# Layer 0's network: key weights staged in sixteen half tiles over two buffers, in the third part and its down part

## The chip, the cores and the metric

The kernel runs on one core of a Trainium2 chip. Its time is device microseconds of one execution; a version is run several times and stands for the median. A core has five engines that run their own instruction streams in order and wait for each other by semaphores: PE (TensorE, matrix products), DVE (VectorE), ACT (ScalarE), POOL (GpSimd) and SP (SyncE). Data moves between memory (DRAM) and the on-chip memory (SBUF) by DMA transfers, which SP, ACT and POOL issue and 16 DMA engines carry out. Products are summed up in PSUM banks.

## The reference

A trunk of two layers over 512 tokens of 1024 features, all float32. Layer 0 is a Mamba-2 mixer and a convolutional feed-forward network (the "network" of the title); then come shared keys and values; layer 1 is differential attention and a second network. What matters here:

```python
def conv_ffn(x, ln_g, up_w, conv_w, conv_b, down_w):
    u = causal_dwconv(rms_norm(x, ln_g) @ up_w, conv_w, conv_b)
    gate, up = u[..., :FFN_DIM], u[..., FFN_DIM:]          # FFN_DIM = 2816
    return (jax.nn.silu(gate) * up) @ down_w

def shared_kv(x, kv_ln_g, kv_w, k_norm_g):
    kv = rms_norm(x, kv_ln_g) @ kv_w
    k = kv[..., :K_DIM].reshape(b, s, ATT_HEADS, 2, ATT_HEAD_DIM)
    v = kv[..., K_DIM:].reshape(b, s, ATT_HEADS, ATT_V_DIM)
    return rms_norm(k, k_norm_g), v

for layer in range(2):
    mix = mamba2_mixer(...) if layer == 0 else diff_attention(x, k_sh, v_sh, ...)
    x = x + mix
    x = x + conv_ffn(x, ...)
```

The gain kv_ln_g of the norm ahead of the keys can be multiplied into the rows of the key half of kv_w beforehand: row k of kv_w times kv_ln_g[k]. That is what is staged here.

## The kernel before

**Products.** A float32 product is made of three PE products of rounded pieces: high piece times high piece, high times low, low times high. For each piece of weights of 128x1024 that comes by DMA (wr_h for the up weights, L177; wr_s, wz, wx for the down weights, L1245 and L1267), ACT copies the high piece wh (L185, L1276) and DVE subtracts to get the low piece wl (L196, L1277). The buffers of wr, wh and wl are three each, so ACT can make the piece of chunk k only when PE has done chunk k - 3.

**Layer 0's network.** Its 22 blocks of 128 gate and 128 up features are worked in three parts, blocks 0 to 5, 6 to 13 and 14 to 21. A plain block is two steps (P), each one chunk of up weights (h_p_0, h_p_1) with 24 matmuls of 128x512; its results are tapped by the convolution (ACT L1066, DVE L1068), pass the Silu on ACT (L1478) and are multiplied on DVE (L1160). In the second part four blocks are worked as doubles, two blocks by seven products (the digits in the list of steps). When a part is done, its share of the down product is made while the next part is under way: the letter D, the *down part*.

```python
PARTS_D = (0, 6), (6, 14), (14, 22)
STEPS = "PPPPPPPPPPPP", "PPDPP51P26P734P51P26734", "PPDPPPPPPPPPPPPPP"
```

The down part of layer 0 (down_features) is seven products, "5126743", each for two halves c of the output, so 14 chunks s_6_0, s_6_1, ... of 24 or fewer matmuls of 128x256. After each product DVE adds the bank ps_s into xT (L1417). For some products the weights are a sum of two quarters of the weight matrix: POOL issues an accumulating DMA (plus, L1238) into the tile wx or wz that the high and low pieces have just been made of.

**Order.** PE's order is written by hand. The other engines' instructions are ordered by a scheduler, which can place an instruction far ahead of the spot where the code emits it, if what it reads is there. `tc.issue_after(x)` keeps what is emitted under it behind the instruction x. SP issues loads in its order, POOL the accumulating ones, ACT the stores of the staged tiles.

**Staging of the key weights.** Layer 1's key products read scaled key weights from a scratch tensor ks in DRAM. Layer 0 fills it: key_weights_in(n) loads two blocks of rows of half the columns of kv_w, 512 KB, into the tile stage (L1005, issued by SP); key_weights_out scales it in place, one ACT instruction per block of rows (L1011), and stores it to ks by a DMA that ACT issues (L1012). There are eight such tiles and one buffer, so each load waits for the store before it. stage() is called after each step of the second and third part, and every other call loads, every other one scales and stores. The scheduler has put all eight tiles earlier: from the end of the mixer's output projection to the middle of the network's first part, from 357 to 438 us of the span.

Of the kernel before, what the change touches and what calls it, by code (L numbers as in the profile page):

```python
# [9 lines left out]
F32 = mybir.dt.float32  # L10
# [8 lines left out]
P = 128  # L19
# [26 lines left out]
def trunk_kernel(ctx: ExitStack, tc, x, ssm_ln_g, ssm_in_w, ssm_conv_w, ssm_conv_b, ssm_dt_bias,  # L46
# [23 lines left out]
    def w_cols(w, k0, nk, c0, ncol):  # L70
        return w[k0 * P:(k0 + nk) * P, c0:c0 + ncol].rearrange("(k p) c -> p k c", p=P), nk, ncol
# [929 lines left out]
        return ks[k0 * P:(k0 + 2) * P, i * 512:(i + 1) * 512].rearrange("(k p) c -> p k c", p=P)  # L1001

    def key_weights_in(pl, n):
        v = pl.tile([P, 1024], F32, tag="stage", name="stage%d" % n, bufs=1).rearrange("p (k c) -> p k c", k=2)
        sync.dma_start(v, w_cols(kv_w, n // 2 * 2, 2, n % 2 * 512, 512)[0])  # L1005
        return n, v

    def key_weights_out(n, v):
        k0, i = n // 2 * 2, n % 2
        for k in range(2):  # L1010
            act.activation(v[:, k], v[:, k], AF.Copy, scale=c2[:, 32 + k0 + k:33 + k0 + k])  # L1011
        act.dma_start(key_weights(k0, i), v)  # L1012

    def bias_ranges(pl, behind):
        pl = pl.rearrange("p a t -> p (a t)")
# [16 lines left out]
    def ffn(l, norm, bp, gnext, nnext):  # L1032
        with (tc.tile_pool(name="ffn_h%d" % l, bufs=1) as hp, tc.tile_pool(name="ffn%d" % l, bufs=1) as fp,
# [129 lines left out]
            def double(p, sides):  # L1163

                uu, ug = [u_tile("u%d%d_%d" % (l, us[0], p)) for _ in range(2)][::1 - 2 * (us[0] % 2)]
                us[0] += 1
                banks = {}
                for m in "5126734":
                    wh, wl = chunk("U%d%s_%d" % (l, m, p))
                    opens = m in "512"  # L1170
                    kind = "y" if m in "53" else "z" if m == "2" else "x"
                    if opens:
                        if m == "1":
                            banks["x"] = [mm_bank("ps_U%s%d_%d_%d" % (m, l, p, b))[:, :256] for b in range(2)]
                        else:
                            t = aux_bank("ps_U%s%d_%d" % (m, l, p))
                            banks[kind] = [t[:, b * 256:(b + 1) * 256] for b in range(2)]
                            banks[kind + "t"] = t.rearrange("p (b t) -> p b t", b=2)
                    ps = banks[kind]
                    hs, ls = up_side(m)  # L1180
                    for b in range(2):
                        cols = slice(b * P, (b + 1) * P)
                        skip = not opens or (b > 0 and m != "1")
                        for k in range(4):
                            pe.matmul(ps[b], wh[:, k, cols], hs[:, k, :], start=not skip and k == 0, stop=False,
                                      skip_group_check=skip)
                            pe.matmul(ps[b], wh[:, k, cols], ls[:, k, :], start=False, stop=False,
                                      skip_group_check=skip)
                        for k in range(4):
                            pe.matmul(ps[b], wl[:, k, cols], hs[:, k, :], start=False, stop=k == 3,  # L1190
                                      skip_group_check=skip)
                        if m == "1":
                            act.activation(ug[:, b, :256], ps[b], AF.Copy)
                        elif m == "6":
                            act.activation(ug[:, b, 256:], ps[b], AF.Copy)
                        elif m == "7":
                            dve.tensor_tensor(out=uu[:, b, 256:], in0=uu[:, b, 256:], in1=ps[b], op=sub)
                        elif m == "4":
                            act.activation(uu[:, b, :256], ps[b], AF.Copy, scale=-1.0)
                    if m == "5":  # L1200
                        act.activation(uu[:, :, 256:], banks["yt"], AF.Copy, scale=-1.0)
                    elif m == "2":
                        dve.tensor_tensor(out=ug[:, :, :256], in0=banks["zt"], in1=ug[:, :, :256], op=ALU.add)
                    elif m == "3":
                        dve.tensor_tensor(out=ug[:, :, 256:], in0=banks["yt"], in1=ug[:, :, 256:], op=ALU.add)
                        ga = [taps(0, p + b, ug[:, b]) for b in range(2)]
                        for b in range(2):
                            act.activation(ga[b], ga[b], AF.Silu)
                    elif m == "4":
                        for b in range(2):  # L1210
                            gated(p + b, ga[b], taps(1, p + b, uu[:, b]), sides)
                    yield
# [193 lines left out]
            def down_features(p0, n, sides, last):  # L1406
# [18 lines left out]
                for m in SEVEN[0]:  # L1425
                    opens = m in "512"
                    for c in range(2):
                        wh, wl = chunk("s0%s_%d_%d" % (m, p0, c))
                        kind = "y" if m in "53" else "z" if m == "2" else "x"
                        if opens:  # L1430
                            banks[kind, c] = (mm_bank if m == "5" else aux_bank)("ps_s%s_%d_%d" % (m, p0, c))
                        v = halves(banks[kind, c])
                        for b in range(2):
                            for low in range(2):
                                for q in range(nq):
                                    h, w = (t[:, side[m], :] for t in sides[q][:2])
                                    cols = slice(b * P, (b + 1) * P)
                                    if low:
                                        pe.matmul(v[:, b], wl[:, q, cols], h, start=False, stop=q == nq - 1,  # L1439
                                                  skip_group_check=not opens or b > 0)  # L1440
                                        continue
                                    pe.matmul(v[:, b], wh[:, q, cols], h, start=opens and q + b == 0, stop=False,  # L1442
                                              skip_group_check=not opens or b > 0)
                                    pe.matmul(v[:, b], wh[:, q, cols], w, start=False, stop=False,  # L1444
                                              skip_group_check=not opens or b > 0)
                        if m == "5":
                            add(c, 1, 1, v, ALU.subtract)
                        elif m == "1":
                            add(c, 0, 0, v)
                        elif m == "2":  # L1450
                            add(c, 0, 0, v)
                            ended(c, 0, 0)
                        elif m == "6":
                            add(c, 0, 1, v)
                        elif m == "7":
                            add(c, 1, 1, v, ALU.subtract)
                            ended(c, 1, 1)
                        elif m == "4":
                            add(c, 1, 0, v, ALU.subtract)
                            ended(c, 1, 0)  # L1460
                        else:
                            add(c, 0, 1, v)
                            ended(c, 0, 1)

            down = down_tokens if nnext is None else down_features
            hooks = state["hooks"]
# [8 lines left out]

            def tapped(p, us):
                ga = taps(0, p, us[0])
                act.activation(ga, ga, AF.Silu)  # L1478
                return ga, taps(1, p, us[1])

            staged = {"n": 0, "at": 0, "v": None}

            def stage():

                staged["at"] += 1
                if staged["v"] and staged["at"] > 1:
                    key_weights_out(*staged["v"])
                    staged.update(v=None, at=0)
                elif not staged["v"] and staged["n"] < KB and staged["at"] > 1:
                    staged.update(v=key_weights_in(fp, staged["n"]), n=staged["n"] + 1, at=0)  # L1490

            def plain(p, sides):

# [7 lines left out]
                gated(p, ga, up, sides)  # L1501
                return ga

            sides = {}
            ps0, ps1 = [], []
            w0 = whole(0, ps0)
            next(w0)
# [49 lines left out]
            for i in range(1, len(parts)):  # L1557
# [23 lines left out]
                for kind, p, step in order:  # L1581
                    if kind == "D":
                        q0, m = parts[i - 1]
                        down(q0, m, [behind[q0 + 2 * j] for j in range(m // 2)], False)
                        gate(sides)
                        continue
                    if p not in gens:
# [2 lines left out]
                    if kind == "P" and step == 1:  # L1590
                        run(gens[p])
                        if p > p0:
                            gate(sides)
                    if not l:
                        stage()
            if staged["v"]:
                key_weights_out(*staged["v"])
            assert l or staged["n"] == KB
            p0, n = parts[-1]
            down(p0, n, [sides[p0 + 2 * j] for j in range(n // 2)], True)  # L1600

# [459 lines left out]
```

## Time and profile before

| | us |
|---|---|
| median of 3 runs | 1311.98 |
| lowest, highest run | 1311.8, 1312.6 |
| the profiled execution | 1313.06 |
| span of its instructions | 1311.4 |

The profile is of one execution. Its time is a little longer than the span from the first to the last instruction that the profile shows; the profiled execution is 1.08 us above the median, and its granted TensorE clock is 0.999 in the mean. Rows of the timeline have the start in us, the duration in us, the engine, the line and the operation, "out<-in", and in brackets the idle time before and what ended it. SPq, ACTq and POOLq rows are the issue of a DMA by that engine. A row of waits has the waiting engine and line, what it waited for, and us in total, times, longest. The chain of waits runs in order of time: start, duration, what. The table of windows has the stretch, its length, the busy time of each engine, the granted clock, the share of the 16 DMA engines and GB/s. A row of a DMA queue has packets, megabytes and its share of the DMA engines.

The staging in the timeline of ACT and SP (starts, us):

| | 1 | 2 | 3 | 4 | 5 | 6 | 7 | 8 |
|---|---|---|---|---|---|---|---|---|
| load issued by SP | 356.73 | 366.30 | 377.08 | 385.91 | 396.79 | 405.18 | 414.42 | 427.17 |
| store issued by ACT | 362.93 | 373.78 | 383.10 | 391.66 | 402.35 | 410.53 | 421.93 | 434.37 |

The down part inside the third part has its matmuls on PE from 574.0 to 614.2 us; before and after it stand the plain steps of the third part.

### The profile page before, as it was taken

To read this page: it belongs to the slowest core of one execution; us is meant where nothing else is said; L and a number is where in the kernel's file an instruction comes from. 1 tells how busy PE (TensorE), PEld (TensorE's weight loads), DVE (VectorE), ACT (ScalarE), POOL (GpSimd) and SP (SyncE) were. 2 spreads that over 40 slices of the span, in tenths; PEclk is the share of its full clock that TensorE was granted. 3 is DMA by queue.
4 is the path that set the end of the run, shared out by engine and by line. 5 is a ranking of instruction groups with operands and counts; after the bars stand their busy time and mean duration, and the time that the engine had idled before them with its cause. 6 is when DMAs were issued, how large, how long until landed. Compare 5 with 4: busy or idle time off the path is not lost.

```text
span 1311.4 us, 19077 instructions
## 1 busy us (share of the span) xinstructions
PE 1302.4 (99%) x7123; PEld 1110.4 (85%) x7123; DVE 1083.1 (83%) x1812; ACT 746.1 (57%) x1234; POOL 184.7 (14%) x212
## 2 busy tenths in 40 slices
PE   9999999999999999999999999999999999999998
PEld 8878888888888798999889888888888889988887
DVE  7989878889869886996778879798789977997776
ACT  6596554743367545653445667777656536643442
POOL 5230200300020411111002310000020030020001
PEclk9999999999999999999999999999999999999999
DMA  7553533532366696778337673222233586565325
GB/s 207 153 154 96 149 100 98 152 96 73 102 192 186 177 218 155 156 150 205 100 97 143 168 157 112 81 65 65 65 105 89 149 203 155 141 123 188 99 61 128
DMA packets 198589, 174.20 MB, mean 133 GB/s; under 512 B 7964, under 2 KB 172192, under 8 KB 198496
## 3 DMA queue, kind: packets, MB, share of 16 engines
q1 hardware_dynamic: 164336, 119.69, 30.7%
q0 software_dynamic: 30704, 47.99, 19.2%
q10 hardware_dynamic: 3456, 5.30, 1.2%
q8 instruction: 56, 0.92, 0.3%
q14 instruction: 37, 0.30, 0.1%
HBM read 166.51 MB, written 6.44 MB: 132 GB/s over the span
## 4 chain that ended last, share of the span: by engine, by line
PE 95%; DVE 3%; ACT 1%; DMA 0%; issue 0%; DVEq 0%; ACTq 0%
PE ps_in L246 5%; PE ps_in L248 5%; PE ps_in L247 5%; PE ps_g L248 5%; PE ps_g L246 4%; PE ps_g L247 4%; PE ps_u L246 4%; PE ps_u L247 4%; PE ps_u L248 4%; PE ps_s L1439 3%; PE ps_s L1444 3%; PE ps_s L1442 3%; PE ps_s L1338 3%; PE ps_s L1341 3%; PE ps_s L1343 3%; PE ps_o L247 2%
## 5 line engine op out<-in xcount | busy, mean ns | idle before, releaser
L246 PE MATMUL ps_in<-xgh,wh_in 128*128 128x512 f32 x304 | 122.9, 404 | 0.0
L196 DVE TENSOR_TENSOR wl_h<-wr_h,wh_h 128x1024 fp32r<-128x1024 f32 x72 | 88.3, 1231 | 41.1 <-ACT wh_h L185 38.3
L248 PE MATMUL ps_in<-xgh,wl_in 128*128 128x512 f32 x304 | 119.8, 394 | 0.0
L247 PE MATMUL ps_in<-xgl,wh_in 128*128 128x512 f32 x304 | 119.2, 392 | 0.0
L248 PE MATMUL ps_g<-xgh,wl_h 128*128 128x512 f32 x288 | 112.7, 391 | 2.8 <-DVE wl_h L196 2.8
L247 PE MATMUL ps_g<-xgl,wh_h 128*128 128x512 f32 x288 | 113.0, 392 | 0.2 <-DVE xgl L1084 0.2
L246 PE MATMUL ps_g<-xgh,wh_h 128*128 128x512 f32 x288 | 113.2, 393 | 0.0
L247 PE MATMUL ps_u<-xgl,wh_h 128*128 128x512 f32 x288 | 112.1, 389 | 0.0
L246 PE MATMUL ps_u<-xgh,wh_h 128*128 128x512 f32 x288 | 112.1, 389 | 0.0
L248 PE MATMUL ps_u<-xgh,wl_h 128*128 128x512 f32 x288 | 112.0, 389 | 0.0
L185 ACT ACTIVATE wh_h<-wr_h 128x1024 fp32r<-128x1024 f32 x72 | 76.2, 1058 | 60.0 <-PE ps_u L247 17.8
L1083 ACT ACTIVATE sh<-vg 128x512 fp32r<-128x512 f32 (+1 forms) x81 | 42.2, 530 | 60.3 <-DVE vg L1160 35.5
L1238 POOL DMA_DIRECT2D wz<-in_ffn_down_w_dram x28 | 33.8, 1265 | 285.6 <-DVE wl_s L1277 131.0
L248 PEld LDWEIGHTS ps_in<-xgh,wl_in 128*128 128x128 f32 x304 | 57.1, 188 | 12.2 <-issue 0.4
L246 PEld LDWEIGHTS ps_in<-xgh,wh_in 128*128 128x128 f32 x304 | 57.2, 188 | 11.7 <-issue 1.3
L248 PEld LDWEIGHTS ps_g<-xgh,wl_h 128*128 128x128 f32 x288 | 54.5, 189 | 14.6 <-DVE wl_h L196 3.2
L247 PEld LDWEIGHTS ps_in<-xgl,wh_in 128*128 128x128 f32 x304 | 57.2, 188 | 11.0 <-issue 0.5
L247 PEld LDWEIGHTS ps_g<-xgl,wh_h 128*128 128x128 f32 x288 | 54.5, 189 | 11.5 <-DVE xgl L1084 0.6
L185 ACT ACTIVATE wh_in<-wr_in 128x1024 fp32r<-128x1024 f32 x39 | 41.2, 1057 | 40.2 <-PE ps_in L247 30.1
L1444 PE MATMUL ps_s<-sl,wh_s 128*128 128x256 f32 x252 | 64.1, 283 | 0.0
L1442 PE MATMUL ps_s<-sh,wh_s 128*128 128x256 f32 x252 | 64.1, 283 | 0.0
L246 PEld LDWEIGHTS ps_g<-xgh,wh_h 128*128 128x128 f32 x288 | 54.4, 189 | 11.0
(518 smaller groups left out, 3809.9 us busy)
## 6 DMA issues: line engine op xcount, KB each, us to landing
wr_h<-in_ffn_up_w_dram SPq DMA_DIRECT2D x60, 512.0 KB, 4.3
wr_in<-in_ssm_in_w_dram SPq DMA_DIRECT2D x40, 512.0 KB, 3.9
wz<-in_ffn_down_w_dram POOLq DMA_DIRECT2D x21, 512.0 KB, 6.8
m<-cumd POOLq DMA_DIRECT2D x16, 512.0 KB, 4.9
wr_out<-in_ssm_out_w_dram SPq DMA_DIRECT2D x16, 512.0 KB, 3.5
wr_s<-in_ffn_down_w_dram SPq DMA_DIRECT2D x13, 512.0 KB, 4.2
wr_h<-in_ffn_up_w_dram SPq DMA_DIRECT2D x24, 256.0 KB, 3.5
wx<-in_ffn_down_w_dram POOLq DMA_DIRECT2D x12, 512.0 KB, 7.4
```

The source lines that it names most:

```text
L185: return act.activation(self.wh[:, :self.n], self.raw[:, :self.n], AF.Copy)
L196: return eng.tensor_tensor(out=self.wl[:, :self.n], in0=self.raw[:, :self.n], in1=self.wh[:, :self.n].bitcast(F32), op=ALU.subtract)
L246: pe.matmul(ps, wh, xh, start=start, stop=False)
L247: pe.matmul(ps, wh, xl, start=False, stop=False)
L248: return pe.matmul(ps, wl, xh, start=False, stop=stop).ins
L1083: act.activation(hi, v, AF.Copy)
L1338: pe.matmul(pss[b], h, ws[q][1][:, cols], start=False, stop=end and q == qs[-1], skip_group_check=more)
L1341: pe.matmul(pss[b], h, ws[q][0][:, cols], start=first and q == qs[0], stop=False, skip_group_check=more)
L1343: pe.matmul(pss[b], w, ws[q][0][:, cols], start=False, stop=False, skip_group_check=more)
L1439: pe.matmul(v[:, b], wl[:, q, cols], h, start=False, stop=q == nq - 1, skip_group_check=not opens or b > 0)
L1442: pe.matmul(v[:, b], wh[:, q, cols], h, start=opens and q + b == 0, stop=False, skip_group_check=not opens or b > 0)
L1444: pe.matmul(v[:, b], wh[:, q, cols], w, start=False, stop=False, skip_group_check=not opens or b > 0)
```

## The change

There are sixteen half tiles of one block of rows and 512 columns (256 KB), over two buffers, in the place of eight tiles over one; the on-chip memory is the same. stage() is called in the third part alone: after each of its sixteen plain steps, and, by the new list `meanwhile`, after each product of its down part. The n-th call scales and stores half tile n - 2 and loads half tile n into the same buffer; scaling and store stand behind state["act"], the last ACT instruction noted at certain places (a product's evacuation in a double, or a Silu). Bytes and scalings are the same; loads and stores are sixteen each instead of eight.

```diff
     def key_weights_in(pl, n):
-        v = pl.tile([P, 1024], F32, tag="stage", name="stage%d" % n, bufs=1).rearrange("p (k c) -> p k c", k=2)
-        sync.dma_start(v, w_cols(kv_w, n // 2 * 2, 2, n % 2 * 512, 512)[0])
+        v = pl.tile([P, 512], F32, tag="stage", name="stage%d" % n, bufs=2)
+        sync.dma_start(v, w_cols(kv_w, n // 2, 1, n % 2 * 512, 512)[0].rearrange("p k c -> p (k c)"))
         return n, v
 
     def key_weights_out(n, v):
-        k0, i = n // 2 * 2, n % 2
-        for k in range(2):
-            act.activation(v[:, k], v[:, k], AF.Copy, scale=c2[:, 32 + k0 + k:33 + k0 + k])
-        act.dma_start(key_weights(k0, i), v)
+        k, i = n // 2, n % 2
+        act.activation(v, v, AF.Copy, scale=c2[:, 32 + k:33 + k])
+        act.dma_start(key_weights(k // 2 * 2, i)[:, k % 2], v)
...
                         if m == "1":
-                            act.activation(ug[:, b, :256], ps[b], AF.Copy)
+                            state["act"] = act.activation(ug[:, b, :256], ps[b], AF.Copy).ins
...
+                    for step in meanwhile:
+                        step()
...
             def tapped(p, us):
                 ga = taps(0, p, us[0])
-                act.activation(ga, ga, AF.Silu)
+                state["act"] = act.activation(ga, ga, AF.Silu).ins
                 return ga, taps(1, p, us[1])
 
-            staged = {"n": 0, "at": 0, "v": None}
+            staged = []
+            count = [0]
 
             def stage():
 
-                staged["at"] += 1
-                if staged["v"] and staged["at"] > 1:
-                    key_weights_out(*staged["v"])
-                    staged.update(v=None, at=0)
-                elif not staged["v"] and staged["n"] < KB and staged["at"] > 1:
-                    staged.update(v=key_weights_in(fp, staged["n"]), n=staged["n"] + 1, at=0)
+                n = count[0]
+                count[0] += 1
+                if 2 <= n < 2 * KB + 2:
+                    with tc.issue_after(state["act"]):
+                        key_weights_out(*staged.pop(0))
+                if n < 2 * KB:
+                    staged.append(key_weights_in(fp, n))
...
                     if kind == "D":
                         q0, m = parts[i - 1]
+                        meanwhile[:] = [stage] if not l and i == len(parts) - 1 else []
                         down(q0, m, [behind[q0 + 2 * j] for j in range(m // 2)], False)
+                        meanwhile[:] = []
                         gate(sides)
...
-                    if not l:
+                    if not l and i == len(parts) - 1:
                         stage()
```

In the changed file the lines of the network stand one further up or down: the scaling is L1010, the store L1011, the pieces wh_s L1275, the taps L1065, the Silu L1479.

What the scheduler makes of it. ACT's order in the first part, around the Silu of block 3 (vg_3; the numbers at the end of a name only tell tiles apart), before:

```order
L185 ACTIVATE wh_h_5_1_4120<-wr_h_5_1_4118 128x1024
L1066 ACTIVATE vg_4_4150<-ps_g_4_4084,cf_90 128x512
L1011 ACTIVATE stage_6225<-stage_6225,c_89 128x512 x2
L1478 ACTIVATE vg_3_4034<-vg_3_4034 128x512
L1012 DMA ks<-stage_6225 128x2x512
L1083 ACTIVATE sh_3959<-vg_3_4034 128x512
```

and now:

```order
L185 ACTIVATE wh_h_5_1_4120<-wr_h_5_1_4118 128x1024
L1065 ACTIVATE vg_4_4150<-ps_g_4_4084,cf_90 128x512
L1479 ACTIVATE vg_3_4034<-vg_3_4034 128x512
L1082 ACTIVATE sh_3959<-vg_3_4034 128x512
L185 ACTIVATE wh_h_6_0_4173<-wr_h_6_0_4171 128x1024
```

The two scalings and the store are gone from between vg_4 and the Silu of vg_3, as are the other staging rows of this part.

ACT's order in the down part inside the third part, from chunk 3 (the second wh_s row with wz_0 or wz_1 is chunk 9 or 8), before:

```order
L1276 ACTIVATE wh_s_6_1_5568<-wz_0_3669 128x1024
L1276 ACTIVATE wh_s_6_0_5601<-wr_s_6_0_5599 128x1024
L1276 ACTIVATE wh_s_6_1_5633<-wr_s_6_1_5631 128x1024
L1276 ACTIVATE wh_s_6_0_5663<-wx_1_3672 128x1024
L1276 ACTIVATE wh_s_6_1_5694<-wx_0_3671 128x1024
```

and now, from the same chunk to chunk 6:

```order
L1275 ACTIVATE wh_s_6_1_5542<-wz_0_3669 128x1024
L1010 ACTIVATE stage_5469<-stage_5469,c_89 128x512
L1010 ACTIVATE stage_5509<-stage_5509,c_89 128x512
L1011 DMA ks<-stage_5469 128x512
L1275 ACTIVATE wh_s_6_0_5579<-wr_s_6_0_5577 128x1024
L1011 DMA ks<-stage_5509 128x512
L1275 ACTIVATE wh_s_6_1_5611<-wr_s_6_1_5609 128x1024
L1010 ACTIVATE stage_5575<-stage_5575,c_89 128x512
L1011 DMA ks<-stage_5575 128x512
L1275 ACTIVATE wh_s_6_0_5645<-wx_1_3672 128x1024
```

Two scalings now stand ahead of chunk 4, and from chunk 6 to chunk 11 one scaling with its store ahead of each piece; the other eight scalings come in the plain steps of blocks 16 to 21.

SP's order over the same stretch, now (before, the same rows stood there without those of stage):

```order
L1266 DMA wr_s_6_0_5773<-in_ffn_down_w_dram 128x4x256
L1005 DMA stage_5575<-in_kv_w_dram 128x512
L1266 DMA wr_s_6_1_5806<-in_ffn_down_w_dram 128x4x256
L1005 DMA stage_5643<-in_kv_w_dram 128x512
L177 DMA wr_h_15_0_5907<-in_ffn_up_w_dram 128x8x128
L1005 DMA stage_5709<-in_kv_w_dram 128x512
L1005 DMA stage_5771<-in_kv_w_dram 128x512
L1005 DMA stage_5839<-in_kv_w_dram 128x512
L1244 DMA wz_1_3670<-in_ffn_down_w_dram 128x4x256
L1005 DMA stage_5905<-in_kv_w_dram 128x512
L1244 DMA wz_0_3669<-in_ffn_down_w_dram 128x4x256
L1005 DMA stage_5971<-in_kv_w_dram 128x512
```

Each of these loads of stage waits for the store of the half tile two before it, and the loads behind it wait with it. The first two loads of stage stand where the first one stood before, ahead of the first part. PE's and POOL's orders are unchanged.

More of the change, by code (lines that the diff above doesn't have):

```diff
@@ L1192, in double @@
                         if m == "1":
-                            act.activation(ug[:, b, :256], ps[b], AF.Copy)
+                            state["act"] = act.activation(ug[:, b, :256], ps[b], AF.Copy).ins
                         elif m == "6":
-                            act.activation(ug[:, b, 256:], ps[b], AF.Copy)
+                            state["act"] = act.activation(ug[:, b, 256:], ps[b], AF.Copy).ins
                         elif m == "7":
@@ L1502, in gate @@
                 return ga
-            sides = {}
+            sides, meanwhile = {}, []
             ps0, ps1 = [], []
@@ L1593, in ffn @@
                             gate(sides)
-                    if not l:
+                    if not l and i == len(parts) - 1:
                         stage()
-            if staged["v"]:
-                key_weights_out(*staged["v"])
-            assert l or staged["n"] == KB
+            assert l or (count[0] >= 2 * KB + 2 and not staged)
             p0, n = parts[-1]
```

## The prediction

> **What bounds the kernel now.** I read the page first: the span, the busy times, the shares of the chain that ended last.
>
> ```profile
> span 1311.4 us, 19077 instructions
> PE 1302.4 (99%) x7123; PEld 1110.4 (85%) x7123; DVE 1083.1 (83%) x1812; ACT 746.1 (57%) x1234; POOL 184.7 (14%) x212
> PE 95%; DVE 3%; ACT 1%; DMA 0%; issue 0%; DVEq 0%; ACTq 0%
> ```
>
> PE is busy 99% of the span and carries 95% of the chain. The diff gives PE the same instructions in the same order, so the time can move in two ways only: a wait of PE goes, or one comes. The view of PE's waits shows those it has, and the same view of everybody's waits from 340 to 440 us shows one that belongs to the staging:
>
> ```profile
> PE ps_g L248 <- DVE wl_h L196: 2.8, 1, 2.8
> ...
> ACT stage L1011 <- DMA stage<-in_kv_w_dram: 8.9, 3, 3.5
> ```
>
> PE's 2.8 us is the largest it has. The chain from 395 to 445 us says where it comes from:
>
> ```profile
> 427.17 5.47 DMA stage<-in_kv_w_dram
> 433.00 1.34 ACT stage L1011 x2
> 434.34 0.53 ACT vg L1478
> 435.50 1.23 DVE wl_h L196
> 436.78 0.50 PE ps_g L248
> ```
>
> The load of the last staged tile lands late, ACT has its two scalings ahead of the Silu of vg, DVE waits for that Silu with the low pieces wl_h queued behind it, and PE waits for wl_h. PE's timeline there, and at an earlier small stall:
>
> ```profile
> 407.03 0.39 PE L246 MATMUL ps_g<-xgh,wh_h 128*128 128x512 f32 x1
> ...
> 407.94 0.40 PE L248 MATMUL ps_g<-xgh,wl_h 128*128 128x512 f32 x1
> ...
> 432.67 0.39 PE L246 MATMUL ps_u<-xgh,wh_h 128*128 128x512 f32 x1
> ...
> 433.57 0.39 PE L247 MATMUL ps_g<-xgl,wh_h 128*128 128x512 f32 x1
> 436.78 0.50 PE L248 MATMUL ps_g<-xgh,wl_h 128*128 128x512 f32 x1 [2.82 <-DVE wl_h L196]
> ...
> 440.75 0.39 PE L246 MATMUL ps_g<-xgh,wh_h 128*128 128x512 f32 x1
> ```
>
> Four starts from 432.67 to 433.57 make the full-speed pitch 0.225 us. From 433.57 to 436.78 are 3.21 us, so 2.98 are lost. The ten starts from 436.78 to 440.75 take 3.97 us instead of 2.25: another 1.72 lost, at 0.40 us apart in the mean. The table of windows shows the granted clock down there:
>
> ```profile
> 430.00:440.00 10.00, 7.18 (x26) 5.52 (x25) 7.33 (x12) 6.04 (x9) 3.34 (x3) 0.86 0.77 227
> ```
>
> (0.86 is the granted clock.) The two starts from 407.03 to 407.94 lose 0.46.
>
> **Gain in the first part.** All eight loads, sixteen scalings and eight stores leave the end of out_proj and the first part; two loads without scalings stay. To be won there: 2.98 + 1.72 + 0.46 = 5.2 us. Next late is DVE: it is without idle time before the stall.
>
> ```profile
> 431.01 1.21 DVE L1084 TENSOR_TENSOR sOl<-wz,sOh 128x1024 fp32r<-128x1024 f32 x1
> 434.89 0.69 DVE L1160 TENSOR_TENSOR vg<-vg,vu 128x512 f32<-128x512 f32 x1 [2.67 <-ACT vg L1478]
> ```
>
> Without the 2.67 the same order brings wl_h's end from 436.73 to 434.06, and PE wants it at 433.57 + 0.225 = 433.80. Some 0.3 us may stay, and the 0.46, whose direct releaser is a DVE instruction, may stay too. So the gain is 4.5 to 5.2; I take 5.2, since ACT's Silu also moves ahead of other work.
>
> **Cost in the down part.** The order shows eight of the sixteen scalings between the pieces of the down part that runs inside the third part, one ahead of each of wh for chunks 6 to 11 (counted from 0) after two together. Each scaling, store, next load into the same buffer, next scaling is a closed ring, and with two buffers three rounds lie between scaling 0 and scaling 6, which stands ahead of wh of chunk 10. ACT works in order: a ring that is late holds wh back, then wl, then PE. ACT's and DVE's rows there:
>
> ```profile
> 576.78 1.04 ACT L1276 ACTIVATE wh_s<-wz 128x1024 fp32r<-128x1024 f32 x1
> ...
> 596.79 1.06 ACT L1276 ACTIVATE wh_s<-wr_s 128x1024 fp32r<-128x1024 f32 x1 [1.82 <-PE ps_s L1444]
> ```
>
> ```profile
> 597.88 1.22 DVE L1277 TENSOR_TENSOR wl_s<-wr_s,wh_s 128x1024 fp32r<-128x1024 f32 x1
> 600.15 0.69 DVE L1417 TENSOR_TENSOR xT<-xT,ps_s 128x512 f32<-128x512 f32 x1 [1.05 <-PE ps_s L1439]
> ```
>
> ```profile
> 602.83 0.28 PE L1442 MATMUL ps_s<-sh,wh_s 128*128 128x256 f32 x1
> ```
>
> PE starts chunk 10 at 602.83 and needs the addition into xT before it, which DVE runs behind wl. Wl may so end at about 602.1 instead of 599.1, and wh may start at 599.8: 3.0 us of slack. What a scaling and its store cost ACT, and how long the ring took where ACT stood waiting for it:
>
> ```profile
> L1011 ACT ACTIVATE stage<-stage,c x16: 705/710/726, 360.6 to 433.6; 128x512 f32<-128x512 f32 x16
> ```
>
> ```profile
> 373.78 0.39 ACTq L1012 DMA_DIRECT2D ks<-stage  x1
> 381.74 1.34 ACT L1011 ACTIVATE stage<-stage,c 128x512 f32<-128x512 f32 x2 [2.02 <-DMA stage<-in_kv_w_dram]
> ...
> 383.57 1.06 ACT L185 ACTIVATE wh_h<-wr_h 128x1024 fp32r<-128x1024 f32 x1 [0.50 <-ACT stage L1011]
> ...
> 391.66 0.37 ACTq L1012 DMA_DIRECT2D ks<-stage  x1
> ...
> 400.98 1.34 ACT L1011 ACTIVATE stage<-stage,c 128x512 f32<-128x512 f32 x2 [3.50 <-DMA stage<-in_kv_w_dram]
> ...
> 421.93 0.37 ACTq L1012 DMA_DIRECT2D ks<-stage  x1
> ```
>
> A store right behind its scaling costs ACT another 0.5 (the wait at 383.57). So scaling 6 must start by 599.8 - 0.71 - 0.5 = 598.6, and scaling 0 runs at about 577.8, behind the piece of 576.78: 20.8 us for three rounds, 6.9 each, 6.2 from a store's issue to the next scaling. The ring took 381.74 - 373.78 = 8.0, 400.98 - 391.66 = 9.3 and 433.00 - 421.93 = 11.1 us for 512 KB. A half tile has 256 KB; what that saves shows in two issue rows of the page's kind:
>
> ```profile
> xT<-in_ffn_down_w_dram SPq DMA_DIRECT2D x6, 512.0 KB, 3.4
> xT<-in_ffn_down_w_dram SPq DMA_DIRECT2D x2, 256.0 KB, 2.7
> ```
>
> 0.7 for each of the two legs: 6.6, 7.9 and 9.7 us. All three are over 6.2. Which rounds meet other transfers? POOL's accumulating ones:
>
> ```profile
> 580.51 1.28 POOL L1238 DMA_DIRECT2D wz<-in_ffn_down_w_dram  x1 [2.36 <-DVE wl_s L1277]
> ...
> 590.77 1.28 POOL L1238 DMA_DIRECT2D wx<-in_ffn_down_w_dram  x1 [0.37 <-DVE wl_s L1277]
> ```
>
> They come in pairs whose data runs in about 579 to 586 and 591 to 597 (an estimate from the queue shares of these stretches). The first round lies wholly beside the first pair, the other two partly beside the second. I take 9.7 for the first and 7.9 for the others: 9.7 + 7.9 + 7.9 - 3 x 6.2 = **6.9 us** that PE waits, in pieces at chunks 6 to 11. The ends: three times 6.6 gives 1.2, three times 9.7 gives 10.5. After the last piece I add the slow clock once, 1.7 as above; nothing to three times that, 5.1, is possible.
>
> How the two kinds share the 16 DMA engines decides between these ends. A down-weight load of SP was issued at 582.0; its landing, and the queues from 582.5 to 585:
>
> ```profile
> DMA to landing us min/median/max: 7.2/7.2/7.2
> ```
>
> ```profile
> q0 software_dynamic: 350, 0.36, 102.2%
> ```
>
> Only POOL's queue moved packets while SP's load was pending. The Trainium skill, "DMA: Bandwidth & Descriptors", section "Queues, rings and completion order", says that each DMA engine goes round-robin between the queues it has work for, packet by packet; by that rule the loads would have had packets here, and this trace disagrees. By the rule the ring would slow to half speed only, which is rival B below.
>
> For the clock the Trainium skill, "TensorE: Matmul & The Clock Gate", section "Part 1: The HAM clock gate", gives half rate after at least one idle window of about 3.4 us. By that, pieces of one to three us would cost no clock, and my sum would be 1.7 lower; the trace shows the clock down after a gap of 3.0.
>
> **SP's queue.** Each stage load of the third part now waits for a store, and SP's later loads stand behind it: wr_s of chunk 11, wr_h_15_0, the two wz (for the final down part), wr_h_15_1, wr_h_16_0. The tightest is wr_h_15_1, behind the ninth stage load, which waits for the store of scaling 6.
>
> ```profile
> wr_h<-in_ffn_up_w_dram SPq DMA_DIRECT2D x60, 512.0 KB, 4.3
> ```
>
> ```profile
> 611.19 1.06 ACT L185 ACTIVATE wh_h<-wr_h 128x1024 fp32r<-128x1024 f32 x1 [1.82 <-PE ps_s L1444]
> ...
> 619.84 1.06 ACT L185 ACTIVATE wh_h<-wr_h 128x1024 fp32r<-128x1024 f32 x1 [2.20 <-PE ps_g L247]
> ```
>
> With scaling 6 late by 6.9, at 605.5, its store goes out at 606.2; about 3 us for its landing (an estimate: between the kernel's 512 KB legs less 0.7) put the load at 609.5 and its landing at 614. ACT wants the piece at 611.19 + 6.9 = 618.1: hidden, with 4 us to spare. If that cover went, PE would lose what comes after 618.
>
> **The last eight scalings** lie among the plain steps of the third part, around 619.84 and after. ACT waits there for PE to free a piece's buffer, not for data; 0.71 + 0.5 fit into idle stretches of 2.2, and PE's 24 matmuls of a step last 24 x 0.225 = 5.4 us, for which ACT owes one piece (1.06) and, now, one scaling. Nothing. Uncovered it would be at most 8 x 1.2 = 9.6. The eight added loads and stores move no more bytes; their issue on SP and ACT is counted in the ring.
>
> **Sum:** -5.2 + 6.9 + 1.7 = +3.4 us. The profiled execution took 1313.06 us around its span of 1311.4, so 1316.5 by its own time; it lies 1.08 above the median of the runs, 1311.98, so the run's median should be **1315.4 us**.
>
> **Rivals.** 0.2% (2.6 us) is about what a measurement of this kernel can tell from no change: under 1309.4 is faster, over 1314.6 slower.
>
> *A, the ring keeps pace* (the other side: faster). Decides at one number: store issue to next scaling at most 6.2 us over three rounds, against 6.6 of the quickest measured round less its two legs. For it: that round held a landing seen late by an ACT busy elsewhere, and the part's DMA has quiet stretches. Against it: POOL's pairs. Then only the gain remains: 1311.98 - 5.2 = 1306.8.
>
> *B, the halves share with POOL's transfers* or slip between them: rounds of about 7.9 all three, 5.1 lost, no clock loss: 1311.98 - 5.2 + 5.1 = 1311.9, no difference.
>
> *C, POOL's queue keeps the halves out entirely*, as from 582.5 to 585, in both pairs: 9.7 each time, 10.5 lost and 1.7 of clock, with the first part's gain at its low end, 4.5: 1311.98 + 7.7 = 1319.7. Slow clock after several pieces would go beyond that.
>
> *That it doesn't do what it says*: one half tile per step and product is meant, but the order crowds eight scalings ahead of chunks 4 to 11, two where one is meant. If PE is not touched by them, this is A.
>
> **How the numbers follow.** Forecast 0.42 (1313 to 1318: slower 0.34, same 0.08); A 0.22 (faster 0.21, same 0.01); B 0.22 (same 0.18, faster 0.02, slower 0.02); C 0.14 (slower 0.13, same 0.01). Faster 0.23, same 0.28, slower 0.49. Range: A's 1306.8 less measurement to C's 1319.7 and a little clock, 1306.5 to 1320.5; both ends are held by the unknown round. Slower alone would be 1314.6 to 1320.5.
>
> **What would show it.** In the changed profile: PE's wait for wl_h at 436 gone and the clock at 1.00 in 430 to 440 (first step). In the down part: ACT's scalings with idle time before them put down to the stage DMA, store issue to scaling of the same buffer 7 to 10 us (second step), PE waits for wl_s or wh_s that sum to about 7 (third), a granted clock under 1 behind them (fourth); no PE wait in the steps after it. I am wrong if rounds take under 6.2, if PE's wait in the first part stays because DVE takes ACT's place, or if a load queued behind a stage load on SP comes late for a chunk.

## The result, and the profile after

| | before | after |
|---|---|---|
| median of 6 runs, us | 1312.29 | 1321.36 |
| lowest, highest | 1311.01, 1312.98 | 1320.01, 1322.89 |
| span of the profiled execution | 1311.4 | 1319.7 |

The change makes the kernel slower by 9.1 us: the ratio is 1.007, with a 95% interval of 1.0057 to 1.0083. The view of PE's waits of the changed kernel (engine and line that waits, what for, us in total, times, longest) has no wait for wl_h any more, and a new one:

```profile
PE ps_s L1441 <- DVE xT L1416: 9.3, 2, 6.0
```

It is in the down part inside the third part. The table of windows (stretch, length, PE, PEld, DVE, ACT, POOL busy, granted clock, DMA share, GB/s) shows that the first part runs at full clock now, and that two stretches of the down part do not:

```profile
430.00:440.00 10.00, 10.00 (x45) 8.27 (x45) 10.00 (x18) 4.49 (x7) 5.45 (x4) 1.00 0.86 177
```

```profile
589.00:596.00 7.00, 2.87 (x24) 2.62 (x22) 1.32 (x3) 1.78 (x2) 1.76 (x2) 1.00 0.84 153
596.00:603.00 7.00, 5.11 (x24) 5.14 (x25) 3.56 (x4) 1.78 (x2) 0.00 (x0) 0.52 0.78 178
603.00:610.00 7.00, 3.67 (x30) 3.50 (x30) 2.15 (x3) 3.82 (x5) 0.00 (x0) 0.99 0.79 269
610.00:614.00 4.00, 4.00 (x23) 4.00 (x23) 2.63 (x3) 0.91 (x2) 0.00 (x0) 0.58 0.78 204
```

PE issues the same 7,123 matmuls in the same order in both kernels, so their starts can be compared one by one. The difference (after less before) moves only at a few places:

| matmul that starts before at | after at | difference of the starts |
|---|---|---|
| 383.1 us, ahead of the first part's stalls | 382.5 | -0.6 |
| 440.75, behind them | 435.0 | -5.7 |
| chunk 8 of the down part, 597.07 | 597.89 | +0.8 (one stall of 6.2) |
| chunk 10, 602.83 | 609.51 | +6.7 (a second one of 3.5, slow clock between them) |
| 605.2, behind the last slow matmul | 613.5 | +8.25 |
| the last one | | +8.3 |

So the first part gave 5.2 us (most of the 0.6 ahead of it arises in the first 10 us of the kernel, before anything that the change touches), and the down part took 14.0: 9.7 in two stalls, 3.9 by the slow clock behind them, and 0.4 in small delays ahead of them. Nothing is lost or won after it. The chain of waits through the down part says what PE waited for (start, duration, what):

```profile
572.74 6.31 DMA ks<-stage
579.11 3.94 DMA stage<-in_kv_w_dram
583.14 0.74 ACT stage L1010
583.90 4.98 DMA ks<-stage
588.94 4.60 DMA stage<-in_kv_w_dram
593.62 0.73 ACT stage L1010
594.38 5.97 DMA ks<-stage
600.42 4.83 DMA stage<-in_kv_w_dram
605.27 0.74 ACT stage L1010
...
608.68 0.69 DVE xT L1416
609.51 0.36 PE ps_s L1441
```

This is the ring, three times round: store, load, scaling. From a store's issue to the next scaling of the same buffer are 10.4, 9.7 and 10.9 us. Scaling 6, ahead of the piece of chunk 10, starts at 605.27. The other buffer's three rounds, read the same way, take 12.4, 9.8 and 10.0 us. ACT stands idle before the scalings of the ring, the longest time before scaling 6 (the bracket has the idle time and what ended it):

```profile
605.27 0.73 ACT L1010 ACTIVATE stage<-stage,c 128x512 f32<-128x512 f32 x1 [6.33 <-DMA stage<-in_kv_w_dram]
```

What the stores wait for shows in the queues. From 573 to 576 us two stores are pending, and from 596 to 598 the store issued at 594.38:

```profile
q0 software_dynamic: 465, 0.47, 102.4%
q10 hardware_dynamic: 2, 0.00, 0.4%
...
ks<-stage ACTq DMA_DIRECT2D x2, 256.0 KB, 6.1
```

```profile
q0 software_dynamic: 396, 0.40, 124.2%
q1 hardware_dynamic: 5, 0.00, 0.6%
```

q0 carries POOL's accumulating transfers, q1 SP's loads, q10 ACT's stores (packets, MB, share of the DMA engines). While one transfer of POOL's runs, the others move next to nothing; behind it they get a turn. POOL issues two transfers of 512 KB here, at 571.12 and 574.77. From 571 to 576 us q0 moves 488 packets, 0.50 MB, which is the first of them, and q10 moves 2. From 576.2 to 577.5 q10 moves 245 packets, 0.45 MB of the two stores' 0.52, and q0 25. From 577.5 to 580.5 it is q0's second transfer again, 403 packets to 26. So a store or load of the ring can lie behind a whole transfer of POOL's, but not behind all of them.

### The profile page after: what moved, and what is told of

Read it like the earlier page. It is cut to its first block, busy times and chain, and to the rows that moved or that the text cites. A ratio compares the mean times of both kernels' runs of the same rounds, so it can differ in the third digit from the quotient of the medians.

```text
span 1319.7 us, 19120 instructions
## 1 busy us (share of the span) xinstructions
PE 1304.2 (99%) x7123; PEld 1113.1 (84%) x7123; DVE 1083.3 (82%) x1812; ACT 748.0 (57%) x1234; POOL 186.1 (14%) x212
## 4 chain that ended last, share of the span: by engine, by line
PE 95%; DMA 2%; DVE 1%; ACT 1%; issue 0%; DVEq 0%; ACTq 0%; SPq 0%
PE ps_in L246 5%; PE ps_in L248 5%; PE ps_in L247 5%; PE ps_g L247 5%; PE ps_g L248 5%; PE ps_u L247 5%; PE ps_g L246 5%; PE ps_u L246 5%; PE ps_u L248 5%; PE ps_s L1337 3%; PE ps_s L1340 3%; PE ps_s L1342 3%; PE ps_o L247 2%; PE ps_o L248 2%; PE ps_o L246 2%; PE ps_s L1441 2%
## 5 line engine op out<-in xcount | busy, mean ns | idle before, releaser
L248 PEld LDWEIGHTS ps_in<-xgh,wl_in 128*128 128x128 f32 x304 | 57.1, 188 | 12.2 <-issue 0.4
L247 PEld LDWEIGHTS ps_u<-xgl,wh_h 128*128 128x128 f32 x288 | 54.1, 188 | 11.2
L248 PEld LDWEIGHTS ps_u<-xgh,wl_h 128*128 128x128 f32 x288 | 54.1, 188 | 11.2
```

The lines of the kernel that those rows point to most:

```text
L247: pe.matmul(ps, wh, xl, start=False, stop=False)
L248: return pe.matmul(ps, wl, xh, start=False, stop=stop).ins
```

## The experiments

Two theories stood against each other. *Ring*: the loss is what the rounds of the ring take too long, because their transfers lie behind others'. *Work*: eight scalings, stores and loads are more than ACT, SP or the DMA engines can do in the down part, whatever they wait for. All ratios below are against the kernel before on the same chip.

**1. Steps only.** The calls in the down part go; two calls behind the last step flush the ring.

```diff
-                        meanwhile[:] = [stage] if not l and i == len(parts) - 1 else []
+                        meanwhile[:] = []
...
+            if not l:
+                stage()
+                stage()
```

> The changed kernel without the calls in the down part: half tiles are loaded, scaled and stored after the plain steps alone, one scaling is left in the down part. Both theories of the loss (ring: each round of store, load and scaling in the down part is longer than the pieces of chunks allow; work: eight scalings, stores and loads crowded into it are too much for ACT, SP or the DMA engines) expect no loss in the down part, and the first part's gain alone: the changed kernel's PE already lies 5.3 us ahead of the kernel before when the down part's stalls begin, so about 1307.0 us (1306.5 to 1308). If the time is over 1310, what was won in the first part is lost again somewhere that neither theory names, such as SP's queue in the plain steps.

Measured: 1312.27 us against 1312.28, ratio 0.9999 (0.999 to 1.0009). But the profiled execution took 1307.76 us with a span of 1306.1, as both theories expected, and its matmuls are 5.4 us ahead to the end; the eleven others took 1311.8 to 1313.4, so the median misses what was expected. The first part's gain is there in the profiled execution, and something takes some 4.5 us in nearly every other one. Experiments 5 and 9 are about that.

**2. Paced.** Each scaling is put behind the newest piece of the down weights, so that one comes every two chunks.

```diff
-                act.activation(wh[:, :n], t[:, :n], AF.Copy)
+                piece = act.activation(wh[:, :n], t[:, :n], AF.Copy).ins
+                if meanwhile:
+                    state["act"] = piece
```

> The changed kernel with one line more: in the down part the last ACT instruction noted is the newest high piece of the down weights, so that one scaling comes every two chunks (5.76 us) and not one every chunk. Ring: the two rounds of the ring get 11.5 us each instead of 5.8, against 10.4, 9.7 and 10.9 us measured from a store to the next scaling plus 0.7 for the scaling: just enough, so no PE wait over 1 us in the down part and 1307 to 1308.5 us. Work: six or seven scalings, stores and loads are still in the down part, so most of the loss of 13.6 us stays: 1316 to 1320 us.

Measured: 1312.6 us, ratio 0.9994 (0.9986 to 1.0003): some 9 us better than the changed kernel with most of the scalings still there, but not 1307. Its waits of PE, and its chain:

```profile
PE ps_g L246 <- ACT wh_h L185: 1.8, 1, 1.8
```

```profile
584.57 6.24 DMA ks<-stage
...
590.86 5.77 DMA stage<-in_kv_w_dram
...
597.47 6.82 DMA ks<-stage
...
604.34 4.28 DMA stage<-in_kv_w_dram
```

The time lies between the two that were expected. The rounds are longer still, 12.2 us from the store at 584.57 to the scaling at 596.72: the expected 11.0 against 11.5 had no margin. In the down part PE loses nothing, with six scalings in it. PE's wait of 1.8 us comes in the first plain step behind it, whose piece of up weights stands on ACT behind the next scaling, and that one waits for its load:

```profile
608.71 0.72 ACT L1010 ACTIVATE stage<-stage,c 128x512 f32<-128x512 f32 x1 [7.33 <-DMA stage<-in_kv_w_dram]
```

By the starts, PE falls back 4.4 us there, with a slow clock behind the wait, and 1.1 later. Most of the loss went when the ring got more time; that speaks against work, and the size was missed.

**3. No accumulating transfers.** POOL's accumulating DMAs for the weights of this down part are left out, so some weight sums are single quarters.

```diff
+                if not l and p0 == 6:
+                    return
                 state["plus"] = pool.dma_start(view(t, nq), source(p0, c, nq, j, i), accum_op=ALU.add).ins
```

> The changed kernel without POOL's accumulating DMAs for the weights of the down part inside the third part; some of its weight sums are thus single quarters. ACT's order is as in the changed kernel. Ring, with legs held up by POOL's packets: rounds of about 2.9 + 3.8 + 0.7 = 7.4 us instead of 11, three of them 1.5 us beyond what is allowed, so PE loses 1 to 4 us there with clock, 1308 to 1311 us. Ring, but with legs that are slow by themselves: rounds stay about 10, 1318 to 1321 us. Work on ACT: unchanged, 1321 us.

Measured: 1310.76 us, ratio 0.999 (0.9981 to 0.9999). In ACT's timeline (start, duration, line, what, idle time before) the three rounds of one buffer are the pairs of a store's issue and the scaling that follows it in the same buffer:

```profile
573.37 0.36 ACTq L1011 DMA_DIRECT2D ks<-stage  x1
...
578.86 0.72 ACT L1010 ACTIVATE stage<-stage,c 128x512 f32<-128x512 f32 x1 [0.51 <-DMA stage<-in_kv_w_dram]
579.61 0.39 ACTq L1011 DMA_DIRECT2D ks<-stage  x1
...
587.14 0.72 ACT L1010 ACTIVATE stage<-stage,c 128x512 f32<-128x512 f32 x1 [3.01 <-DMA stage<-in_kv_w_dram]
587.89 0.33 ACTq L1011 DMA_DIRECT2D ks<-stage  x1
...
594.61 0.72 ACT L1010 ACTIVATE stage<-stage,c 128x512 f32<-128x512 f32 x1 [2.86 <-DMA stage<-in_kv_w_dram]
```

They take 5.5, 7.5 and 6.7 us instead of 10.4, 9.7 and 10.9; the other buffer's take 7.5, 6.8 and 8.8 instead of 12.4, 9.8 and 10.0. The first two stores, issued into the stretch that q0 filled above, now land in 2.0 us and not 6.1, and the loads behind them in 3.3:

```profile
ks<-stage ACTq DMA_DIRECT2D x2, 256.0 KB, 2.0
stage<-in_kv_w_dram SPq DMA_DIRECT2D x2, 256.0 KB, 3.3
```

PE still waits in the down part, 2.3 us:

```profile
PE ps_s L1443 <- ACT wh_s L1277: 1.3, 1, 1.3
...
PE ps_s L1443 <- DVE xT L1418: 1.0, 1, 1.0
```

Eight scalings, eight stores and loads in the same order on ACT and SP, and most of the loss is gone with the transfers they lay behind (2.8 us instead of 14.0, by the starts; the expectations counted 13.6): as far as ACT and SP go, the work theory falls. What is left is the ring's too: the 8.8 us round ends with the scaling ahead of chunk 11, where PE has the second of its waits. This run also takes bytes from the 16 DMA engines, so by itself it does not tell whether the legs waited because a transfer of POOL's had its turn first or because the engines were full. For the first speak the queues from 571 to 580 us above, and experiment 2, where PE loses nothing in the down part with all of POOL's transfers and six of the eight scalings in it.

**4. No early stores.** The first eight half tiles aren't stored; each of the last eight is stored to two places.

```diff
-        act.dma_start(key_weights(k // 2 * 2, i)[:, k % 2], v)
+        if n >= KB:
+            for r in (k, k - KB // 2):
+                act.dma_start(key_weights(r // 2 * 2, i)[:, r % 2], v)
```

> The changed kernel without the stores of the first eight half tiles; each of the last eight is stored to two places instead. The scalings and loads of the down part stay, the ring there has no store leg. Ring: a round is a load and a scaling, 4 to 5 plus 0.7, under the 6.9 allowed, so no loss or at most 2 us: 1307 to 1309.5 us. Work: eight scalings and loads are still between the pieces, most of the loss stays: over 1316 us.

Measured: 1311.99 us, ratio 0.9998 (0.9989 to 1.0007). Without its store leg the ring costs PE 2.5 us of waits in the down part (3.2 by the starts):

```profile
PE ps_s L1443 <- ACT wh_s L1277: 2.5, 2, 2.3
```

It lies between the two expectations, nearer to ring. The scheduler packed the scalings closer here, two more ahead of chunk 5, and POOL's transfers still delay the loads; so this run tells less than the third.

**5. Steps only, two calls earlier.** As 1, with the first two calls ahead of the third part in the place of the flush behind it.

```diff
                 order = list(up_order(i))
+                if not l and i == len(parts) - 1:
+                    stage()
+                    stage()
```

> As steps only, but with the first two calls before the third part begins, so that each half tile comes two steps (11 us) earlier and the last scaling lies before the final down part. The profiled execution of steps only took 1307.8 us, but its eleven others 1311.8 to 1313.4 with a lower mean clock, about 3 us of stall and one slow window more; its last scaling stood ahead of a piece of the final down part at 693.9 us, behind a load that was issued at 691 just as POOL's accumulating transfers of that part went out. If that load is what comes late in the others (ring, at a second place): 1307 to 1308 us here in the median, with a clock of 1.0. If the stall is elsewhere: about 1312 us again.

Measured: 1307.5 us (1307.04 to 1307.97), ratio 0.9962 (0.995 to 0.9975): faster than both kernels, in every execution.

**6. Sparse.** As 2, with calls after three products only.

```diff
-                    for step in meanwhile:
+                    for step in meanwhile if m in "527" else []:
```

> As paced, but with calls after three of the seven products of the down part only (5, 2 and 7), so that a buffer's store and next load have two products, four chunks, of time and more. Ring: no wait of PE in the down part, and the staging ends before the final down part: 1307 to 1308.5 us. If one scaling with store and load among the chunks costs PE by itself: three or four of them remain, 1309 us or more.

Measured: 1307.34 us (1307.07 to 1308.51), ratio 0.9962 (0.9948 to 0.9975). Four scalings with their stores stand in the down part, and PE has no wait there; its largest behind the start of the kernel is this one, in the other layer:

```profile
PE ps_s L1342 <- DVE vu L1067: 0.4, 1, 0.4
```

**7. Halves alone.** The kernel before with half tiles over two buffers, called where it called (the functions key_weights_in and key_weights_out of the change, stage() without issue_after).

> The kernel before with half tiles over two buffers alone, called after each step of the second and third part as before; the scheduler puts all of it at the end of the output projection and in the first part again. There POOL issues no accumulating transfers, so the ring's legs are free of them. If the halves by themselves shorten ACT's waits there (legs 0.7 shorter, one load under the other half's scaling): the stall of 3.0 and the slow clock behind it go in part, 1307 to 1311 us. If the halves bring nothing: 1312 us; if sixteen stores and loads cost more than eight: over 1314 us.

Measured: 1318.37 us, ratio 1.0045 (1.0031 to 1.0058). The half tiles by themselves make the old place worse. The stall for wl_h is gone there too, but earlier ones come; PE's waits:

```profile
PE ps_g L247 <- DVE xgl L1083: 3.2, 2, 2.2
PE tr_nf L552 <- DVE nacc_f L605: 3.1, 1, 3.1
...
PE al_nf L562 <- DVE tr_nf L305: 1.1, 1, 1.1
```

The chain to them runs over loads and stores of stage. That sixteen scalings, each with a wait of its own, stand ahead of more of ACT's urgent work than eight pairs do is argued from the order, not shown.

**8. The place alone.** Full tiles over one buffer, called in the third part and its down part.

> The kernel before with the new place alone: eight full tiles over one buffer, called in the third part and its down part only. In the down part the order has two scalings each ahead of chunks 3, 7, 10 and 13. Ring: a round is store, load and two scalings, over 10.4 + 1.4 + 0.7 = 12.5 us with POOL's transfers, three of them 37.5 against 10 chunks of 2.88 and 3.0 of slack, 31.8: 5.7 lost, plus 1.7 to 3.4 of slow clock, 1314 to 1316 us. Work on ACT alone: about as the changed kernel, 1321 us.

Measured: 1320.58 us, ratio 1.0062 (1.0049 to 1.0076), 5 us more than expected. In the down part PE falls back 10.0 us (expected 7.4 to 9.1). The first round takes 13.9 us from its store to the next scaling, 13.7 of them for the two legs, where the expectation had allowed 11.8; PE's wait follows:

```profile
572.72 7.08 DMA ks<-stage
...
579.86 6.66 DMA stage<-in_kv_w_dram
```

```profile
PE ps_s L1442 <- ACT wh_s L1276: 6.3, 2, 5.6
```

Another 3.6 are lost behind the down part, where I had expected nothing: 1.9 up to 665 us, around the last scalings at 660, and 1.7 from 698 to 711, when the staging is over. What causes the second is not shown. The number alone is that of the work theory. The waits in the down part are the ring's: ACT has stood idle for a load before the scalings ahead of that wait.

```profile
599.97 1.33 ACT L1011 ACTIVATE stage<-stage,c 128x512 f32<-128x512 f32 x2 [8.53 <-DMA stage<-in_kv_w_dram]
```

**9. Steps only, once more.** For a profile of one of its longer executions.

> The kernel of steps only once more, for a profile of one of its longer executions (eleven of twelve took 1311.8 to 1313.4 us, the profiled one 1307.8). Ring at a second place: PE level with the short execution up to about 694 us, then one stall of 2 to 4 us in the final down part, behind ACT's last scaling, whose load lands 3 us or more later than the 2.9 us of the short execution, with a slow clock window behind it. Elsewhere: PE falls back at another time, with no wait for the stage load there.

Measured: 1312.19 us. PE is level with the short execution up to 690 us, then waits once in the final down part. PE's wait, the chain to it, and the window behind it:

```profile
PE ps_s L1438 <- DVE wl_s L1276: 2.8, 1, 2.8
```

```profile
681.27 6.93 DMA stage<-in_kv_w_dram
688.28 0.38 ACT stage L1010
...
688.91 0.77 ACT vu L1065
...
693.50 1.15 DVE wl_s L1276
694.69 0.89 PE ps_s L1438 x4
```

```profile
695.00:700.00 5.00, 5.00 (x32) 5.00 (x30) 5.00 (x8) 2.23 (x3) 2.58 (x2) 0.66 0.68 130
```

A stage load issued at 681.27, between two accumulating transfers that POOL issues at 679.45 and 682.13, takes 6.9 us. In the short execution the same load goes out at 680.07, takes 4.5, and the two scalings run together at 684.1. From 681 to 682.5 us only SP's queue moves packets there (71), and here only POOL's (128): the load that starts 1.2 us later finds POOL's transfer ahead of it. The scaling of 688.28 is the last but one, not the last as expected; otherwise this is what was expected of the ring at a second place. By the starts 3.0 us of stall and 1.6 of slow clock, less 0.3 made up behind them, are the difference to the short execution.

## Why the prediction was wrong

The direction and the mechanism were right: slower, by the ring in the down part, more than the first part gives. The time was outside the range, at 1321.4 against 1315.4 (1306.5 to 1320.5).

- *Gain in the first part, 5.2 us.* Right: 5.2 in the starts, 4.7 at the stall of 436.78 with its slow clock and 0.5 at the small one of 407.6; no wait of PE for wl_h, a clock of 1.00. DVE did not take ACT's place.
- *The order on ACT, two scalings and then one ahead of each piece, and PE behind it.* Right, but for the size of the pieces: the wait was thought to come in pieces at chunks 6 to 11, and it came in two stalls, ahead of chunks 8 and 10. The wait named by the profile is for the addition into xT, which DVE runs behind wl_s.
- *Cost in the down part: the rounds of 9.7 + 7.9 + 7.9 us.* This is the step that failed, as a term mis-sized. They took 10.4 + 9.7 + 10.9 = 31.0, not 25.5. Its premise was that the rounds measured in the first part show what the ring takes, less 0.7 for each leg, and that only the first round meets POOL's transfers wholly. There were no accumulating transfers beside those rounds of the first part; without them the same three rounds take 5.5, 7.5 and 6.7 (experiment 3), near the quick end of what was measured. With them each grew by 2.2 to 4.9, and the last, taken to meet them only in part, was the longest. Allowed were 18.6, so scaling 6 came 12.4 late instead of 6.9; by chunk 10 PE had lost 9.7 of that in stalls, 2.4 by the slow clock between them and 0.4 in small delays.
- *Slow clock once, 1.7.* Also too small: 3.9 us. The stall of 6.2 was followed by a slow clock up to 603 us (0.52 from 596 to 603), and the second by a shorter stretch (0.58 from 610 to 614). The text named this as possible and left it out of the sum.
- *The last eight scalings and SP's queue: nothing.* Right for the changed kernel: the difference of the starts does not move behind 613 us. In steps only, where the staging runs on into the final down part, the ring costs 4.4 us there in the execution of experiment 9.
- *Rival C, POOL's queue keeps the halves out.* It was the nearer one, with 9.7 for each round, 1319.7, and POOL's queue did hold the halves up (465 packets against 2). But it did not keep them out entirely: they had a turn between two of POOL's transfers. The prediction took the row of 582.5 to 585 as evidence against queues that take turns; the changed kernel's trace shows turns, a whole transfer at a time. It too was short by the clock and by the third round. It had been given 0.14, since I let the accumulating transfers decide about one round in three, although the row of 582.5 to 585 showed their queue alone.

The half tiles, whose saving I had counted on, were no gain in the old place (experiment 7), and in the new one no gain clear of the noise (experiment 8's ratio of 1.0062 with full tiles against 1.007). The gain comes from leaving the old place, and it is kept where the ring stays clear of most accumulating transfers (experiment 5) or has time for them (experiment 6). Whether full tiles would do as well there was not tested.

## What to carry to other kernels

A ring of load, work and store over few buffers has a round trip, and it has to be priced in the stretch where it will run, with the transfers of that stretch: here 5.5 to 8.8 us without the other queue's accumulating transfers and 9.7 to 12.4 beside them. An in-order engine that serves both the ring and the critical path turns each late round into a stall of the critical path; give such a ring clearly more than its round trip (in experiment 6 a buffer had 16.5 and 22.2 us from a store to its next scaling in the down part, PE had no wait there, and the time is 1307.3 us where the changed kernel takes 1321.4; the 11.5 us of experiment 2 were not enough), and end it ahead of the next crowded stretch. One profile can lie on the lucky side of such a race: compare its time with the other executions before reading it.

## What the runs showed of the hardware

From 573 to 576 us POOL's queue moved 465 packets and ACT's stores 2, with both stores pending, and the stores moved when POOL's transfer of 512 KB was through, ahead of its next one, which had been issued at 574.77. In experiment 9 the order is the same: POOL's queue alone from 681 to 682.5, then SP's load (101 packets to 45 from 684.5 to 686), then POOL's second transfer (458 to 14 from 686.5 to 689). That the queues always take turns by whole transfers is not shown by these two places. A slow clock of some 6.8 us (596.3 to 603.2) came behind the 6.2 us stall, and one of 3.4 behind the 3.5 us stall of the changed kernel, behind the 3.0 us stall of the kernel before and behind that of 3.0 us in experiment 9. Waits of 1.3 and 1.0 us left the mean clock at 1.0 in experiment 3, and two of 2.5 together in experiment 4. In experiment 7 a stall of 3.2 us at 382 to 385 us is followed by full clock, and the slow clock comes only at 407.3, behind a later stall of 2.4. Experiment 2, with a wait of 1.8 us and two short ones, has this in its table of windows:

```profile
612.00:616.00 4.00, 4.00 (x12) 3.12 (x11) 1.96 (x3) 0.00 (x0) 1.45 (x2) 0.57 0.86 125
```

The length of a stall alone does not tell whether the clock drops.
